# Encoder trunk on one core: the planner's TensorE starts later than the other engines, and transposes are queued later

## The chip, the cores and the metric

The kernel runs on one core of one Trainium2 chip. The metric is the device time of one execution in microseconds (us). A profiled execution has a time of its own, and beside it a span, which runs from the first to the last instruction.

The engines are called by their names in the profile: PE is TensorE (matrix products and transposes), DVE is VectorE, ACT is ScalarE, POOL is GpSimd, and SP is SyncE, which here issues nearly all transfers.

## The reference, cut to what matters

```python
for layer in range(DEPTH):                       # DEPTH = 2
    y = ab_mixer(...) if layer % 2 == 0 else cd_mixer(...)
    x = layer_norm(DN_ALPHA * x + y, ln_mix_g[layer], ln_mix_b[layer])
    f = swiglu(x, w_gate, w_up, w_down)          # (silu(x @ w_gate) * (x @ w_up)) @ w_down
    x = layer_norm(DN_ALPHA * x + f, ln_ffn_g[layer], ln_ffn_b[layer])
```

x has 256 tokens of 2048 float32 values. The feed-forward part (SwiGLU) is 5632 wide. The first layer's mixer joins a neighbourhood attention and a gated recurrence, the second layer's joins a pooling mixer and grouped-query attention. Each mixer has one projection in and one out.

## The kernel before, in words

**Tiles and products.** The 256 tokens are two tiles of 128, called tok 0 and tok 1. A float32 product is made of three matmuls (`mm3`, or `product` in the planner): each operand is split into a high part and a low part, and the three are high by low, high by high, and low by high. Their rows read `whi,xTl`, `whi,xTh` and `wlo,xTh`. Weights come from memory as pieces of 128 x 1024 values: SP issues the load into one of four `raw` buffers, ACT casts it to `whi`, and DVE takes the difference into `wlo`. One piece then serves twelve matmuls (two slices of the contraction, two tok, three products). Activations are transposed on PE (four matmuls against `ident` for 512 values of each of 128 tokens), and the result is split in the same way: ACT writes `xTh` or `yTh`, DVE writes `xTl` or `yTl`.

**Stages of a layer.** Mixer, projection out, normalisation; then `ffn`: gate and up of the first of eleven chunks of 512 hidden values (`mm_chunk`, with the SiLU on ACT at L838 and the gated product on DVE at L845, written into a view of the tile `y4h`); then `inner`; then the down projection of the last two chunks; then the normalisation that feeds the next layer.

**The planner.** `inner` computes the other ten chunks and the down projection of nine. It doesn't issue instructions as it goes, but collects operations in a `Plan`, each with its engine, its size, what it reads and writes, and the buffers (`Place`) it takes. `run` then simulates the four engines with a table of costs in ns (L88): each operation on PE is due when the ones ahead of it on PE are through, counted from zero (L150), its helpers are due that much earlier, and at each step each engine takes, among the operations that are ready, the one that is due first (L172). The order found is issued and pinned per engine with `keep_in_program_order`. The planner's clock starts at zero for every engine (L160), and it does not know of the stage ahead of it, whose instructions are still running on all engines when the first planned ones are queued.

Nine of the chunks go in units, in which six of the eight pairs of contraction slices take a form with fewer products and more additions. Its sums of activations are made by `make_forms`: two additions of `xTh` and `xTl` into `rs` (L572), four small ones into `z` (L591), then the split into `f0h` and `f0l` (L531, L535). Its sums of weights are made by `load_seven` from loads of twice the size (`rs<-in_gu`) into `sh` and `sl`.

**The end of the units.** The last unit's gated values g (ACT L664, DVE L668) of both tok are transposed outside the planner by `transpose4`, on the third and fourth piece's turn (`before`); neither they nor the products there are pinned, and the order of before has them ahead of the first product. The two banks `acc` and the two banks `mx` of the output's first half are seeded with the residual by ACT (`seed`, L413), since the first matmul adds to what stands there.

**The normalisation and the next mixer.** The second half of the output is computed tok by tok (`tok_major`). After tok 0, `norm` (L427 to L451) makes the new activations in `res`, and `flip` transposes them in four steps (L477, L478), which are not issued at once but kept in `pending`. The next `tok_major` chunk takes one step ahead of each of its pieces from piece number `FIRST_STEP` (5) on, and the rest after its last piece. Tok 0's steps are so laid into the products of tok 1, and tok 1's into the first chunk of the second layer's mixer (`cd_mixer`, its chunk 0 for keys and values). The constants of that mixer are loaded behind the last weight load of this chunk; the scale of the query norm, `nwq`, is multiplied on DVE at L1198.

Of the kernel before, what the change touches and what calls it, by code (L numbers as in the profile page):

```python
# [64 lines left out]
CD_OUT_GROUPS = (2, 0, 3, 1)  # L65
FIRST_STEP = 5
HELD = 6
FREE = 7
# [5 lines left out]
HALF = "psspsspssp"  # L74
SOON = 4000


# [12 lines left out]
class Plan:  # L90
# [11 lines left out]

    def op(self, engine, size, fn, reads=(), writes=(), times=1, lag=0, due=0):
        cost = 50 if engine == "SP" else self.COST[engine][size] * times
        i = len(self.ops)
        needs = {}
        for x in reads:
            if x in self.wrote:
                needs[self.wrote[x]] = 1
            self.read.setdefault(x, []).append(i)  # L110
        for x in writes:
            if x in self.wrote:
                needs[self.wrote[x]] = 1
            for r in self.read.pop(x, ()):
                needs.setdefault(r, 0)
            self.wrote[x] = i
        for place, _ in (*reads, *writes):
            if isinstance(place, Place) and i not in place.users:
                place.users.append(i)
        needs.pop(i, None)  # L120
        first = [p for p, _ in writes if isinstance(p, Place)]
        self.ops.append((engine, cost, size, fn, needs, first, lag, due))
        return i

    def run(self):
# [23 lines left out]
        assert len(order) == n  # L149
        due, t = [1e12] * n, 0  # L150
        pe = [i for i in range(n) if ops[i][0] == "PE"]
# [6 lines left out]
        due = [d - o[7] for d, o in zip(due, ops)]  # L158
        ready, left = [0.0] * n, [len(x) for x in needs]
        free = dict.fromkeys(("PE", "ACT", "DVE", "SP"), 0.0)  # L160
        open_ = {e: {i for i in range(n) if ops[i][0] == e and not left[i]} for e in free}
        queue, at, start, bus = 0, 0.0, [0.0] * n, 0.0
        for _ in range(n):
            best = None
            for e in free:
                if e == "PE":
                    picks = [pe[queue]] if queue < len(pe) and not left[pe[queue]] else []
                else:
                    picks = open_[e]
                if picks:  # L170
                    t = max(free[e], min(ready[i] for i in picks))
                    c = min((t, due[i], i) for i in picks if ready[i] <= t)  # L172
                    best = c if best is None else min(best, c)
            t, _, i = best
            e, cost, _, _, _, _, lag, _ = ops[i]
            open_[e].discard(i)
            queue += e == "PE"
            start[i], free[e] = t, t + cost
            end = t + cost
            if e == "SP":  # L180
                bus = max(t + 1600, bus) + ops[i][2] / 360 * 1000
                end = bus + 300
            for j in users[i]:
                x = end if needs[j][i] else t + cost
                ready[j] = max(ready[j], x + (130 + lag * needs[j][i] if ops[j][0] != e else 0))
                left[j] -= 1
                if not left[j]:
                    open_[ops[j][0]].add(j)
# [11 lines left out]
def trunk(ctx: ExitStack, tc: tile.TileContext, a, out):  # L200
# [93 lines left out]

    def mm_chunk(halves, lhs, outs, tok_major=False, after=None, before=None, seeded=False):

# [18 lines left out]
        if tok_major:  # L315
# [5 lines left out]
            for tok in range(NT):  # L321
                for i in range(n):
                    if pending and i >= FIRST_STEP:
                        step()
# [7 lines left out]
        else:  # L332
            for i, half in enumerate(halves):
                src = half[0]
                loaded.append(load_half(src, before(i) if before else ()))
                for kks in ((0,), (1,)) if before and i == 0 else ((0, 1),):
                    for tok in range(NT):
                        mms(i, tok, kks=kks)
            if after:
# [40 lines left out]
    def transpose4(src, hi, lo, ahead_by=0):  # L380
        t = trp()
        for k in range(4):
            transpose(t[:, k * P : (k + 1) * P], src[:, k * P : (k + 1) * P], ident)
        v = t.rearrange("p (k t) -> p k t", k=4)
# [131 lines left out]
    def inner(layer, sp, xT, y4, res):  # L516
# [44 lines left out]
        def make_forms(n, seven):  # L561
# [5 lines left out]
            for t in range(NT):  # L567
# [8 lines left out]
                    (),  # L576
                    [(xs, t)],
                )
            both = [(xs, 0), (xs, 1)]
# [80 lines left out]

        def gated(tok, gate, up, y):

            g = tile_of(sp, [P, NCH], f"g{tok}", 1)
            plan.op("ACT", 512, lambda: [nc.scalar.activation(g.get(), gate.get(), AF.Silu)], [(gate, 0)], [(g, 0)])  # L664
# [34 lines left out]

        def unit(w, y, down):  # L700

# [64 lines left out]
            for tok in range(NT):  # L766
                gated(tok, b[f"c{tok + 1}1"], b[f"c{tok + 1}2"], y)

# [49 lines left out]
        for units, chunks in ROUNDS:  # L818
            down = down_steps(chunks, [ys[c] for c in chunks], chunks[0] == 0)
            for c in units:  # L820
                ys[c] = new_y()
                unit(w[c], ys[c], down)
            assert next(down, None) is None
# [4 lines left out]
    def ffn(layer, xT, res, mix_pool, close_mix, keep, last):  # L828
# [54 lines left out]

        mm_chunk(some((0, 1), [(ci, j, j) for ci in range(2) for j in range(2)]), yl, outs, after=both, before=before, seeded=True)
        if cdp:
# [15 lines left out]

        mm_chunk(some((2, 3), [(ci, j, j) for j in (2, 3) for ci in range(2)]), yl, ends, tok_major=True, after=after, seeded=True)
        rings.pop()
# [310 lines left out]
    def cd_mixer(mp, consts, xT, yT):  # L1214
# [102 lines left out]
        for c, (kind, _) in enumerate(cd_plan()):  # L1317
            outs = [acc() for _ in range(NT)]
            mm_chunk([(a["cd_in"][c, n], two(2 * n)) for n in range(8)], lhs, outs, tok_major=(c == 0))
            if c == 0:  # L1320
# [174 lines left out]
```

## Time and profile before

| | |
|---|---|
| time, median of 3 runs | 2172.07 us (2170.62 to 2173.68) |
| time of the profiled execution | 2174.74 us |
| span of the profiled execution | 2173.0 us |
| mean granted TensorE clock | 0.994 of full speed |
| PE busy | 2136.8 us, 98% of the span |
| DVE busy | 1768.5 us, 81% |
| ACT busy | 1239.2 us, 57% |
| moved by DMA | 477.25 MB, 220 GB/s over the span |

A row of the timeline reads: start, duration, engine, line of the kernel, operation, out<-in, count, and in square brackets how long the engine was idle before it and what it waited for. Matmuls are pipelined: one of 128x512 has a row of 0.39 us and the next starts 0.23 us after it. A row `PE acc L557 <- ACT whi L531` in the list of waits says that the matmuls of L557 into `acc` waited for the casts of L531 into `whi`, and gives the total in us, how many times, and the longest. PEclk is the granted clock.

### The profile page before, as it was taken

Reading aid. Unit: us, or ns where it says so; the run is one execution under the profiler, and the core shown is the slowest. Engines: PE = TensorE matmul, PEld = TensorE weight load, DVE = VectorE, ACT = ScalarE, POOL = GpSimd, SP = SyncE. Lnnn points to the kernel's source line nnn. Section 1 sums busy time; section 2 is a strip of 40 time slices with the busy share of each in tenths; the row PEclk is TensorE's granted clock in tenths of the full one; section 3 lists DMA queues with packets and bytes.
Section 4 is the critical chain, followed back from the end, with each engine's and each line's share of the span. In section 5 each row is a group of like instructions: output and inputs, shape, how many; then the busy total and the mean of one; then the engine's idle time right before and its main releaser. Section 6 shows DMA issues by size and latency. Waiting matters only on the chain.

```text
span 2173.0 us, 27222 instructions
## 1 busy us (share of the span) xinstructions
PE 2136.8 (98%) x9856; PEld 1772.6 (82%) x9856; DVE 1768.5 (81%) x2226; ACT 1239.2 (57%) x1618; POOL 37.4 (2%) x43
## 2 busy tenths in 40 slices
PE   9999999999899999999999999998999999999998
PEld 7888888888788888888888788887888888888886
DVE  6885688666789999999996776675899999999976
ACT  6445534554456666666676564443566666666763
POOL 0000001000000000000000000000000000000000
PEclk9999999999999999999999999999999999999999
DMA  8555545584567777777775563554777767777754
GB/s 295 162 163 178 169 139 182 189 292 145 180 241 254 259 253 253 250 251 247 257 242 194 210 225 121 202 190 145 259 253 259 255 245 260 249 248 257 255 184 173
DMA packets 118614, 477.25 MB, mean 220 GB/s; under 512 B 13904, under 2 KB 16976, under 8 KB 103376
## 3 DMA queue, kind: packets, MB, share of 16 engines
q1 hardware_dynamic: 118480, 475.53, 63.6%
q8 instruction: 77, 1.26, 0.2%
q14 instruction: 57, 0.47, 0.1%
HBM read 473.37 MB, written 2.10 MB: 219 GB/s over the span
## 4 chain that ended last, share of the span: by engine, by line
PE 92%; DVE 4%; DMA 2%; issue 1%; ACT 1%; SPq 0%; DVEq 0%; ACTq 0%
PE un L557 33%; PE acc L398 32%; PE acc L557 19%; PE mx L398 4%; PE mx L1047 1%; PE tr L240 1%; PE un L240 1%; DMA raw<-in_down 1%; DVE wlo L244 1%; DMA rs<-in_gu 1%; DVE wlo L535 1%; ACT whi L243 0%; DMA raw<-in_cd_in 0%; PE mx L1093 0%; PE mx L1308 0%
## 5 line engine op out<-in xcount | busy, mean ns | idle before, releaser
L531 ACT CAST whi<-raw 128x1024 fp32r<-128x1024 f32 x356 | 372.2, 1050 | 211.8 <-PE acc L557 98.5
L244 DVE TENSOR_TENSOR wlo<-raw,whi 128x1024 fp32r<-128x1024 f32 (+1 forms) x297 | 360.7, 1224 | 154.9 <-ACT whi L243 152.4
L535 DVE TENSOR_TENSOR wlo<-raw,whi 128x1024 fp32r<-128x1024 f32 x356 | 430.5, 1220 | 66.4 <-ACT whi L531 62.5
L243 ACT CAST whi<-raw 128x1024 fp32r<-128x1024 f32 (+1 forms) x297 | 309.4, 1049 | 300.6 <-PE acc L398 186.7
L398 PE MATMUL acc<-whi,xTl 128*128 128x512 f32 x736 | 293.1, 398 | 5.4 <-ACT whi L243 5.1
L398 PE MATMUL acc<-whi,xTh 128*128 128x512 f32 x736 | 290.5, 395 | 0.0
L398 PE MATMUL acc<-wlo,xTh 128*128 128x512 f32 x736 | 288.1, 394 | 0.0
L557 PE MATMUL acc<-whi,yTl 128*128 128x512 f32 x576 | 225.8, 392 | 0.0
L557 PE MATMUL acc<-wlo,yTh 128*128 128x512 f32 x576 | 224.4, 390 | 0.0
L557 PE MATMUL acc<-whi,yTh 128*128 128x512 f32 x576 | 224.1, 389 | 0.0
L531 ACT CAST sh<-z 128x1024 fp32r<-128x1024 f32 x108 | 113.8, 1053 | 126.7 <-DVE z L627 73.2
L557 PE MATMUL un<-whi,xTl 128*128 128x512 f32 x460 | 180.9, 393 | 1.2 <-ACT un L731 1.1
L557 PE MATMUL un<-whi,xTh 128*128 128x512 f32 x460 | 179.2, 389 | 0.0
L557 PE MATMUL un<-wlo,xTh 128*128 128x512 f32 x460 | 179.1, 389 | 0.0
L398 PEld LDWEIGHTS acc<-whi,xTl 128*128 128x128 f32 x736 | 139.2, 189 | 33.0 <-ACT whi L243 5.8
L398 PEld LDWEIGHTS acc<-wlo,xTh 128*128 128x128 f32 x736 | 139.1, 189 | 28.4 <-DVE wlo L244 0.5
L398 PEld LDWEIGHTS acc<-whi,xTh 128*128 128x128 f32 x736 | 139.3, 189 | 26.5
L535 DVE TENSOR_TENSOR sl<-rs,sh 128x1024 fp32r<-128x1024 f32 x108 | 131.7, 1219 | 26.2 <-ACT sh L531 26.2
L531 ACT CAST sh<-rs 128x1024 fp32r<-128x1024 f32 x108 | 113.3, 1049 | 42.2 <-PE un L557 27.7
L627 DVE TENSOR_TENSOR z<-rs 128x1024 f32<-128x1024 f32 x108 | 131.7, 1220 | 1.8 <-DMA rs<-in_gu 1.0
L535 DVE TENSOR_TENSOR sl<-z,sh 128x1024 fp32r<-128x1024 f32 x108 | 131.6, 1218 | 0.0
L557 PEld LDWEIGHTS acc<-wlo,yTh 128*128 128x128 f32 x576 | 108.1, 188 | 22.7
(301 smaller groups left out, 3957.2 us busy)
## 6 DMA issues: line engine op xcount, KB each, us to landing
raw<-in_gu SPq DMA_DIRECT2D x244, 512.0 KB, 4.9
rs<-in_gu SPq DMA_DIRECT2D x108, 1024.0 KB, 4.9
raw<-in_down SPq DMA_DIRECT2D x176, 512.0 KB, 4.3
raw<-in_ab_in SPq DMA_DIRECT2D x127, 512.0 KB, 4.1
raw<-in_cd_in SPq DMA_DIRECT2D x40, 512.0 KB, 4.6
raw<-in_ab_out SPq DMA_DIRECT2D x32, 512.0 KB, 4.2
raw<-in_cd_out SPq DMA_DIRECT2D x32, 512.0 KB, 4.2
bias<-in_na_bias SPq DMA_DIRECT2D x32, 64.0 KB, 3.9
```

Of the source, the lines that this page charges most:

```text
L240: return nc.tensor.transpose(o, src, eye)
L243: nc.scalar.copy(hi, src)
L244: return nc.vector.tensor_tensor(lo, src, hi.bitcast(F32), op=sub).ins
L398: ins = nc.tensor.matmul(o, lhs[a], rhs[b], start=start and n == 0, stop=stop and n == 2, **more)
L531: plan.op("ACT", size, lambda: [nc.scalar.copy(high(), src())], reads, [(hi, at)])
L535: lambda: [nc.vector.tensor_tensor(low(), src(), high().bitcast(F32), op=sub)],
L557: yield nc.tensor.matmul(o.get(), x[i], r[j], start=begin and n == 0, stop=end and n == 2, **kw)
L627: lambda: [tt(g(), r()[:, 0:3:2], r()[:, 3:4].to_broadcast([P, 2, NCH]), op=add)],
L1047: nc.tensor.matmul(m[:, 2 * h + s, :], kk[:, h, s * P : (s + 1) * P], qq[:, h, r * P : (r + 1) * P], start=True, stop=True,)
```

## The change

The lines of the kernel move by two or three; L398 becomes L400, for instance.

```diff
+LATER = 7
+LEAD = 14000
...
-    def op(self, engine, size, fn, reads=(), writes=(), times=1, lag=0, due=0):
+    def op(self, engine, size, fn, reads=(), writes=(), times=1, lag=0, due=0, after=0):
...
-        due, t = [1e12] * n, 0
+        due, t = [1e12] * n, LEAD
...
-        ready, left = [0.0] * n, [len(x) for x in needs]
-        free = dict.fromkeys(("PE", "ACT", "DVE", "SP"), 0.0)
+        ready, left = [float(o[8]) for o in ops], [len(x) for x in needs]
+        free = {"PE": float(LEAD), "ACT": 0.0, "DVE": 0.0, "SP": 0.0}
...
-    def mm_chunk(halves, lhs, outs, tok_major=False, after=None, before=None, seeded=False):
+    def mm_chunk(halves, lhs, outs, tok_major=False, after=None, before=None, seeded=False, first_step=FIRST_STEP, pinned=0):
...
-                    if pending and i >= FIRST_STEP:
+                    if pending and i >= first_step:
...
-                        mms(i, tok, kks=kks)
+                        mms(i, tok, i < pinned, kks=kks)
...
     def transpose4(src, hi, lo, ahead_by=0):
-            transpose(t[:, k * P : (k + 1) * P], src[:, k * P : (k + 1) * P], ident)
+            tc.keep_in_program_order(transpose(t[:, k * P : (k + 1) * P], src[:, k * P : (k + 1) * P], ident))
...
     def make_forms(n, seven):       # the two additions into rs
+                    after=LEAD,
...
-        def gated(tok, gate, up, y):
-            g = tile_of(sp, [P, NCH], f"g{tok}", 1)
+        def gated(tok, gate, up, y, last=False):
+            g = edge_place(1 + tok) if last else tile_of(sp, [P, NCH], f"g{tok}", 1)
...
-                unit(w[c], ys[c], down)
+                unit(w[c], ys[c], down, c == LAST[1])
...
-        mm_chunk(some((0, 1), ...), yl, outs, after=both, before=before, seeded=True)
+        mm_chunk(some((0, 1), ...), yl, outs, after=both, before=before, seeded=True, pinned=4)
...
-        mm_chunk(some((2, 3), ...), yl, ends, tok_major=True, after=after, seeded=True)
+        mm_chunk(some((2, 3), ...), yl, ends, tok_major=True, after=after, seeded=True, first_step=LATER)
...
-            mm_chunk([(a["cd_in"][c, n], two(2 * n)) for n in range(8)], lhs, outs, tok_major=(c == 0))
+            mm_chunk([(a["cd_in"][c, n], two(2 * n)) for n in range(8)], lhs, outs, tok_major=(c == 0), first_step=LATER)
```

It has three parts. The first starts the planner's PE at 14,000 ns (`LEAD`) and its ACT, DVE and SP at zero, and holds the additions into `rs` back to the same time. The second puts the last unit's gated values into views of `y4h` instead of a buffer of their own, keeps their transposes in program order, and pins the products of the first four pieces of the last down projection, so that the transposes stand behind the first two pieces' products. The third makes the steps of `flip` begin at piece 7 instead of 5, in the second half of the down projection and in the second mixer's first chunk. The number of matmuls, casts and DVE instructions is as before.

**Place 1, the start of the planned operations, layer 0 (the same in layer 1), DVE.** L244 is the split of the stage ahead, `wlo` of L535 the planned one. Before:

```order
L244 TENSOR_TENSOR wlo<-raw,whi 128x1024 x8
L845 TENSOR_TENSOR y4h<-y4h,mx 128x512 x2
L572 TENSOR_TENSOR rs<-xTh_3818,xTl_3820 128x512
L572 TENSOR_TENSOR rs<-xTh_3819,xTl_3821 128x512
L591 TENSOR_TENSOR z<-rs 128x256
L591 TENSOR_TENSOR z<-z,rs 128x256
L591 TENSOR_TENSOR z<-rs 128x256
L591 TENSOR_TENSOR z<-rs,z 128x256
L572 TENSOR_TENSOR rs<-xTh_3818,xTl_3820 128x512
L535 TENSOR_TENSOR f0l<-z,f0h 128x1024
L535 TENSOR_TENSOR wlo<-raw,whi 128x1024 x3
```

Now:

```order
L246 TENSOR_TENSOR wlo<-raw,whi 128x1024 x8
L537 TENSOR_TENSOR wlo<-raw,whi 128x1024 x4
L848 TENSOR_TENSOR y4h<-y4h,mx 128x512 x2
L574 TENSOR_TENSOR rs<-xTh_3818,xTl_3820 128x512
L574 TENSOR_TENSOR rs<-xTh_3819,xTl_3821 128x512
L594 TENSOR_TENSOR z<-rs 128x256
```

Four planned splits now stand ahead of the gated product and of the additions. The casts on ACT move with them. Before:

```order
L243 CAST whi<-raw 128x1024 x8
L838 ACTIVATE y4h<-acc 128x512
L531 CAST f0h<-z 128x1024
L531 CAST whi<-raw 128x1024 x5
L531 CAST f1h<-z 128x1024
```

Now:

```order
L245 CAST whi<-raw 128x1024 x8
L841 ACTIVATE y4h<-acc 128x512
L533 CAST whi<-raw 128x1024 x4
L533 CAST f0h<-z 128x1024
L533 CAST whi<-raw 128x1024 x3
L533 CAST f1h<-z 128x1024
```

Four of the planned casts have moved ahead of `f0h`. On SP ten loads of `raw` now stand ahead of the first load of `rs` instead of eight.

**Place 2, the end of the units, layer 0 (the same in layer 1), PE.** `un` are the last unit's products, `tr` the transposes of its gated values, `acc` and `mx` the output's first half. Before:

```order
L557 MATMUL un<-wlo,xTh_3819 128x512
L240 MATMUL tr<-ident,g_9854 128x128 x4
L240 MATMUL tr<-ident,g_9862 128x128 x4
L398 MATMUL acc<-whi,yTl 128x512
L398 MATMUL acc<-whi,yTh 128x512
```

Now, at the point where the transposes went (24 matmuls into `acc` stand between the last `un` and the first row):

```order
L400 MATMUL acc<-whi,yTh 128x512
L400 MATMUL acc<-wlo,yTh 128x512
L242 MATMUL tr<-ident,y4h 128x128 x4
L400 MATMUL mx<-whi,yTl 128x512
L400 MATMUL mx<-whi,yTh 128x512
```

The first transposes have moved behind 24 matmuls, and the second behind 12 more. On ACT, L413 is the seed of a bank. Before:

```order
L243 CAST whi<-raw 128x1024 x2
L664 ACTIVATE g_9854<-un 128x512
L664 ACTIVATE g_9862<-un 128x512
L243 CAST whi<-raw 128x1024
L413 ACTIVATE acc<-res_3802 128x512
L413 ACTIVATE mx<-res_3802 128x512
```

Now:

```order
L245 CAST whi<-raw 128x1024 x2
L667 ACTIVATE y4h<-un 128x512 x2
L245 CAST whi<-raw 128x1024 x4
L415 ACTIVATE acc<-res_3802 128x512
L415 ACTIVATE mx<-res_3802 128x512
```

Four casts of weights instead of one stand between the SiLU and the first seed.

**Place 3, the start of the second layer's mixer, DVE.** `xTl` are the low parts of the transposed activations of tok 0, L421 the statistics of tok 1. Before:

```order
L451 TENSOR_TENSOR res_3802<-res_3802,bet 128x512 x2
L244 TENSOR_TENSOR wlo<-raw,whi 128x1024 x2
L478 TENSOR_TENSOR xTl_9896<-tr,xTh_9894 128x512
L244 TENSOR_TENSOR wlo<-raw,whi 128x1024
L478 TENSOR_TENSOR xTl_9896<-mx,xTh_9894 128x512
L478 TENSOR_TENSOR xTl_9896<-tr,xTh_9894 128x512
L421 BN_STATS st_9899<-mx 128x6
L244 TENSOR_TENSOR wlo<-raw,whi 128x1024
L478 TENSOR_TENSOR xTl_9896<-mx,xTh_9894 128x512
L427 BN_AGGR mv<-st_9899 128x2
L1198 TENSOR_SCALAR nwq<-nwq 128x128
```

Now:

```order
L453 TENSOR_TENSOR res_3802<-res_3802,bet 128x512
L246 TENSOR_TENSOR wlo<-raw,whi 128x1024 x2
L480 TENSOR_TENSOR xTl_9894<-tr,xTh_9892 128x512
L1201 TENSOR_SCALAR nwq<-nwq 128x128
L423 BN_STATS st_9897<-mx 128x6
L246 TENSOR_TENSOR wlo<-raw,whi 128x1024
L480 TENSOR_TENSOR xTl_9894<-mx,xTh_9892 128x512
L480 TENSOR_TENSOR xTl_9894<-tr,xTh_9892 128x512
L429 BN_AGGR mv<-st_9897 128x2
L480 TENSOR_TENSOR xTl_9894<-mx,xTh_9892 128x512
```

The product of `nwq` has moved up from behind the last `xTl` to behind the first. On SP the load of `nwq` no longer stands behind a load of weights.

More of the change, by code (lines that the diff above doesn't have):

```diff
@@ L121, in op @@
         first = [p for p, _ in writes if isinstance(p, Place)]
-        self.ops.append((engine, cost, size, fn, needs, first, lag, due))
+        self.ops.append((engine, cost, size, fn, needs, first, lag, due, after))
         return i
@@ L174, in run @@
             t, _, i = best
-            e, cost, _, _, _, _, lag, _ = ops[i]
+            e, cost, _, _, _, _, lag, _, _ = ops[i]
             open_[e].discard(i)
@@ L698, in whole, with unit @@
                 gated(tok, gate[tok], up[tok], y)
-        def unit(w, y, down):
+        def unit(w, y, down, last):
             run = lambda: next(down, None)
@@ L766, in unit @@
             for tok in range(NT):
-                gated(tok, b[f"c{tok + 1}1"], b[f"c{tok + 1}2"], y)
+                gated(tok, b[f"c{tok + 1}1"], b[f"c{tok + 1}2"], y, last)
         def down_steps(chunks, ys, start):
@@ L882, in before @@
             return ()
-        mm_chunk(some((0, 1), [(ci, j, j) for ci in range(2) for j in range(2)]), yl, outs, after=both, before=before, seeded=True)
+        mm_chunk(some((0, 1), [(ci, j, j) for ci in range(2) for j in range(2)]), yl, outs, after=both, before=before, seeded=True, pinned=4)
         if cdp:
@@ L900, in after @@
                 norms[0](tok, nxt, out if last else None, {j: ends[tok][j] for j in (2, 3)})
-        mm_chunk(some((2, 3), [(ci, j, j) for j in (2, 3) for ci in range(2)]), yl, ends, tok_major=True, after=after, seeded=True)
+        mm_chunk(some((2, 3), [(ci, j, j) for j in (2, 3) for ci in range(2)]), yl, ends, tok_major=True, after=after, seeded=True, first_step=LATER)
         rings.pop()
```

## The prediction, made before the change was run

> **What bounds the kernel now.** I read the busy times of the page first, then the chain that ended last, then PE's list of waits.
>
> ```profile
> PE 2136.8 (98%) x9856; PEld 1772.6 (82%) x9856; DVE 1768.5 (81%) x2226; ACT 1239.2 (57%) x1618; POOL 37.4 (2%) x43
> ...
> PE 92%; DVE 4%; DMA 2%; issue 1%; ACT 1%; SPq 0%; DVEq 0%; ACTq 0%
> ...
> PE acc L557 <- ACT whi L531: 11.5, 2, 5.7
> PE acc L398 <- ACT whi L243: 5.1, 2, 4.8
> PE tr L240 <- DVE res L451: 3.0, 2, 2.3
> PE tr L240 <- DVE g L668: 2.4, 2, 1.2
> PE acc L557 <- DVE wlo L535: 1.5, 2, 0.8
> ```
>
> PE is never idle for long, and 92% of the chain is PE's. The number of matmuls doesn't change, so the change can move the time only through PE's holes and what follows them. The second wait row is at the kernel's start, which the change leaves alone. The other four are the change's three places: 11.5 + 1.5 us where planned work begins (twice, once in each layer), 2.4 where the units end (twice), 3.0 where the second mixer begins.
>
> **Place 1, the planned start: a gain.** PE in layer 0, then in layer 1:
>
> ```profile
> 556.88 0.39 PE L398 MATMUL mx<-wlo,xTh 128*128 128x512 f32 x1
> 562.99 0.80 PE L557 MATMUL acc<-whi,xTl 128*128 128x512 f32 x1 [5.72 <-ACT whi L531]
> 564.99 0.80 PE L557 MATMUL acc<-wlo,xTh 128*128 128x512 f32 x1 [0.78 <-DVE wlo L535]
> ...
> 577.69 0.39 PE L557 MATMUL acc<-wlo,xTh 128*128 128x512 f32 x1
> 577.92 1.03 PE L240 MATMUL un<-ident,y4h 128*128 128x128 f32 x8
> ...
> 1500.81 0.39 PE L398 MATMUL mx<-wlo,xTh 128*128 128x512 f32 x1
> 1506.94 0.80 PE L557 MATMUL acc<-whi,xTl 128*128 128x512 f32 x1 [5.74 <-ACT whi L531]
> ...
> 1521.00 1.03 PE L240 MATMUL un<-ident,y4h 128*128 128x128 f32 x8
> ```
>
> Matmuls at full rate start 0.227 us apart (577.69 to 577.92). From the last `mx` to the transposes there are 48 planned matmuls (four pieces of twelve), 10.88 us at that rate. Layer 0 takes 577.92 − 557.11 = 20.81, layer 1 1521.00 − 1501.04 = 19.96. So 9.9 and 9.1 are lost, 19.0 in all: 13.0 in waits (11.5 + 1.5 in the list), the rest in matmuls at half rate behind them. The other engines in layer 0:
>
> ```profile
> 534.25 34.78 SPq L541 DMA_DIRECT2D raw<-in_gu  x8
> ...
> 560.95 1.04 ACT L531 CAST f0h<-z 128x1024 fp32r<-128x1024 f32 x1 [20.89 <-DVE z L591]
> 561.90 3.88 ACT L531 CAST whi<-raw 128x1024 fp32r<-128x1024 f32 x4
> ...
> 563.72 3.49 DVE L535 TENSOR_TENSOR wlo<-raw,whi 128x1024 fp32r<-128x1024 f32 x3
> ...
> 550.00:560.00 10.00, 7.27 (x33) 5.68 (x31) 3.24 (x6) 0.00 (x0) 0.00 (x0) 0.99 0.00 0
> 560.00:570.00 10.00, 6.23 (x14) 4.45 (x15) 9.68 (x15) 5.60 (x6) 0.00 (x0) 0.50 0.36 120
> ```
>
> The casts that PE lacks stood behind `f0h` on ACT, which slept 20.89 us until `z` was there; `z` needs the gated product, and that needs the last `mx`. The loads were not the reason: in 550 to 560 DMA moved nothing (last column 0). In the new order the four casts and four splits stand ahead of the gated product, behind loads that began at 534.25 and need only buffers that the up matmuls free as they go. A cast takes 0.97 (3.88 / 4), a split 1.16 (3.49 / 3); four fit between 540 and 557, while ACT is idle. In layer 1 the fourth buffer comes free only with the last `mx`, so its split ends near 1501.0 + 0.97 + 1.16 = 1503.2, but the fourth piece is wanted 3 x 2.72 = 8.2 us after the start, at 1509.2. No wait is left at the start: **−19.0**.
>
> What is late next is DVE. PE comes 9.9 and 9.1 us earlier, but the gated product and the additions behind it gain only the four splits (4.6 us) in layer 0, and only 2.3 in layer 1, where the product now waits for the late fourth split. DVE is left 5.3 and 6.8 us further behind PE than before. What covers that is its idle time at the end of the first 65 us of planned work:
>
> ```profile
> 606.00:624.00 18.00, 18.00 (x85) 14.99 (x84) 11.00 (x12) 9.04 (x10) 0.00 (x0) 1.00 0.58 192
> ```
>
> DVE (third pair) is busy 11.0 of 18.0: 7.0 us of idle, which holds 5.3, and just holds 6.8. Until then every buffer margin must bear the lag; pieces five to eight, by the same cast and split times from z's end, come 1.5 to 2.8 us before PE wants them. I take nothing off and keep the loss of it as a rival.
>
> **Place 2, the units' end: a loss, twice.** Layer 0, PE, ACT and SP, and the landings of `raw` from 1162 to 1190:
>
> ```profile
> 1173.61 0.60 PE L240 MATMUL tr<-ident,g 128*128 128x128 f32 x4
> 1175.40 0.63 PE L240 MATMUL tr<-ident,g 128*128 128x128 f32 x4 [1.19 <-DVE g L668]
> 1175.79 0.47 PE L398 MATMUL acc<-whi,yTl 128*128 128x512 f32 x1
> 1176.10 0.39 PE L398 MATMUL acc<-whi,yTh 128*128 128x512 f32 x1
> ...
> 1171.09 0.60 ACT L664 ACTIVATE g<-un 128x512 f32<-128x512 f32 x1 [0.76 <-PE un L557]
> 1172.35 1.05 ACT L243 CAST whi<-raw 128x1024 fp32r<-128x1024 f32 x1 [0.67 <-DMA raw<-in_down]
> 1173.31 0.59 ACT L413 ACTIVATE acc<-res 128x512 f32<-128x512 f32 x1
> ...
> 1169.12 1.69 SPq L281 DMA_DIRECT2D raw<-in_down  x2
> ...
> DMA to landing us min/median/max: 3.2/4.3/5.5
> ```
>
> Call E the end of the last unit product, 1173.61. Before, two transposes and the wait for g put the first `acc` matmul at E + 2.18. Now that matmul is first and needs only its pieces and its seed. But the seed, done by 1173.9 before, stands behind four casts instead of one. The fourth cast's load is the second of the two issued from 1169.12, at 1169.12 + 1.69 − 0.33 = 1170.5; with 4.3 it lands at 1174.8, the cast ends at 1175.7, the seed at 1176.3: a hole of 2.7 us (2.45 with the landing of 3.2, 4.0 with 5.5). The transposes then cost their 2 x 0.36 later on, so one end loses 2.7 − 2.18 + 0.72 = 1.2.
>
> A hole of this length may also cost the clock. Nearest rows: the hole of 1.8 us between 1173.61 and 1175.40 was followed by full rate (the next matmul's row has 0.39 us); the rows of place 3 show one of 2.26 and more, ahead of 1231.91, in a window with a clock of 0.83, about 1.5 us lost. So the price is 0 to 1.5, and 2.7 is nearer to the second: I take 1.3. Two ends: 2 x (1.2 + 1.3) = **+5.0** (bounds 2 and 8).
>
> **Place 3, the second mixer: a small gain.** PE, DVE, SP, and the window 1230 to 1240:
>
> ```profile
> 1208.55 0.39 PE L398 MATMUL acc<-whi,yTl 128*128 128x512 f32 x1
> ...
> 1216.24 0.63 PE L240 MATMUL tr<-ident,res 128*128 128x128 f32 x4 [0.72 <-DVE res L451]
> ...
> 1222.56 0.50 PE L398 MATMUL acc<-whi,xTl 128*128 128x512 f32 x1 [0.22 <-DVE xTl L478]
> ...
> 1231.91 0.76 PE L240 MATMUL tr<-ident,res 128*128 128x128 f32 x4 [2.26 <-DVE res L451]
> ...
> 1221.82 0.68 DVE L478 TENSOR_TENSOR xTl<-tr,xTh 128x512 fp32r<-128x512 f32 x1
> ...
> 1228.23 0.23 DVE L1198 TENSOR_SCALAR nwq<-nwq 128x128 f32<-128x128 f32 x1 [0.90 <-DMA nwq<-in_d_q_norm]
> ...
> 1210.64 0.33 SPq L281 DMA_DIRECT2D raw<-in_cd_in  x1
> ...
> 1230.00:1240.00 10.00, 8.09 (x37) 6.72 (x38) 7.06 (x11) 5.49 (x10) 0.00 (x0) 0.83 0.35 122
> ```
>
> Against the 0.36 of an undisturbed group of transposes, the three rows with waits cost 0.9, 0.6 and 2.4 us; at the clock of 0.83 another 1.5 go: 5.4 in all. Two pieces of six matmuls are 2 x 1.36 = 2.7 us by which both sets of steps move back, more than the 0.72 and 2.26 waited, so those two vanish. But three of tok 0's four steps now stand right ahead of the mixer's first product, which needs the first `xTl`. If P is the start of tok 1's products (1208.55), PE gets there at P + 48 x 0.227 + 4 x 0.36 = P + 12.3. The first `xTl` keeps as many splits ahead of it as before, when it ended at 1222.4 = P + 13.9, and the statistics of tok 1 now stand ahead of it behind the split of the load issued at 1210.64 (P + 2.1): P + 13.6 to P + 16.3, with a landing of 4 to 7 us, the casts and splits behind it. The new wait is 1.3 to 4.0; I take 2.2, nearer the row of before, 0.8 for the clock behind it (0 to 1.5), and 0.4 for `nwq` (0 to 1.4: its load is issued 0.4 earlier, but it is queued four DVE instructions ahead of where it waited 0.90). −5.4 + 3.4 = **−2.0** (bounds −4 and +1.5).
>
> **The sum.** −19.0 + 5.0 − 2.0 = −16.0. The profiled execution took 2174.74, 2.67 over the median; 2174.74 − 16.0 = 2158.7 in its terms, and against the median 2172.07 − 16.0 = **2156**.
>
> **The rivals.**
>
> *The new holes leave the clock alone.* Then place 2 costs 2 x 1.2 = 2.4, and place 3 gives −5.4 + 2.6 = −2.8: −19.0 + 2.4 − 2.8 = −19.4, so 2152.7. For it speaks the hole of 1.8 at 1175.40, after which nothing was slow; against it the hole before 1231.91. The Trainium skill, "TensorE: Matmul & The Clock Gate" (Why this matters for your kernels), asks for no idle gaps over about 3 us, by which holes of 2.7 would pass; the clock of 0.83 behind 1231.91 doesn't agree.
>
> *The seeds come in time.* If PE goes straight from the unit into `acc`, each end gains 2.18 − 0.72 = 1.5, and with nothing new at place 3 the sum is −19.0 − 3.0 − 5.4 = −27.4: 2144.7. The four casts ahead of the seed in the new order speak against it.
>
> *DVE takes the head start back.* If DVE's idle 7.0 us come too late for a buffer that it frees, only what DVE itself gained stays: −4.6 − 2.3 + 5.0 − 2.0 = −3.9, so 2168.2. For it: DVE is busy 9.68 of 10 in 560 to 570. Against: among the waits of PE over half a microsecond, those above, none is for DVE's work inside the units.
>
> *Slower: the transposes' low parts wait for a late load, at both ends.* In the new order the first `yTl` of the last chunk stands on DVE behind seven splits, the last of them of the eleventh piece. That piece's buffer is freed by the seventh piece's split, which follows the six seeds: 1175.7 + 6 x 0.53 + 0.97 + 1.16 = 1181.0 = E + 7.4; with a landing of 4.3, 0.97 and 1.16 for cast and split and 0.6 for itself `yTl` is there at E + 14.5, just when PE (E + 2.7, 48 matmuls, two transposes: E + 14.3) wants it. Each us that this load is later goes straight to PE. Landings of 4.3 + 6.7 = 11.0 make two losses of 6.7 and two clocks of 1.3, 16.0: from there on the kernel is slower. At 12 it is 2172.07 − 16.0 + 2 x (7.7 + 1.3) = 2174. In 1162 to 1190 no landing is over 5.5, but half a chunk later:
>
> ```profile
> DMA to landing us min/median/max: 3.1/4.6/10.9
> ```
>
> That the change doesn't do what it says is out: the order's rows show the four casts and splits ahead.
>
> **How the numbers follow.** My forecast 0.60, clock untouched 0.22, seeds in time 0.05, DVE 0.08, slower 0.05. The forecast alone spans −16.0 with +3 at place 2, and −2 to +3.5 at place 3, from 2151 to 2162. The range 2149 to 2164 takes in the second case and part of the DVE case, with 0.15 to 0.2 left out. A change of under 0.2% (4.3 us) can't be told from none here, so faster means below 2167.7: the first three cases and half of the fourth, 0.91; the same 0.05, slower 0.04.
>
> **What would show it.** Right: the row `acc <- whi` of the planned start is gone from the waits, 48 matmuls take some 11 us after the last `mx`; at the units' end the first `acc` matmul waits 2 to 3 us for a cast or a seed (L415), with a lower clock behind it; the first matmul of the second mixer waits for `xTl`, and the row `tr <- res` is gone. Wrong: waits in the units for DVE's `wlo`, `z` or `sl` in the first 100 us of planned work; a wait for `yTl` at the end; or the old hole, shorter, at the start.

## The result, and the profile after

| | before | changed |
|---|---|---|
| median | 2172.39 us (2170.62 to 2173.68) | 2156.01 us (2155.03 to 2157.57) |
| ratio | | 0.9926 (0.9909 to 0.9943) |
| median, in a later group of runs | 2175.81 us | 2159.01 us |
| ratio there | | 0.9921 (0.9907 to 0.9934) |
| span of the profiled execution | 2173.0 us | 2153.9 us |

The change makes the kernel 16.4 us faster, 2156.0 us where 2156 was forecast. The total is the forecast's; two of its terms are not, as the places show, so that the close agreement of the total is partly luck.

The page and PE's list of waits of the changed kernel; in the list, line 415 is the seed:

```profile
PE 2130.5 (99%) x9856; PEld 1768.5 (82%) x9856; DVE 1767.9 (82%) x2226; ACT 1239.1 (58%) x1618; POOL 41.9 (2%) x43
...
PE acc L400 <- ACT whi L245: 5.6, 3, 4.8
PE acc L400 <- ACT acc L415: 5.0, 2, 2.6
PE un L559 <- ACT un L734: 1.0, 2, 0.5
PE un L242 <- DVE g L671: 0.4, 2, 0.2
PE acc L400 <- DVE xTl L480: 0.2, 1, 0.2
```

The 11.5 and 1.5 us of the planned start are gone, and so are the waits for `res` and for g ahead of `tr`. One row is new: 5.0 us for the seed.

**Place 1.** PE, ACT and DVE in layer 0, and the window that answers to the one in which DVE was idle for 7 us:

```profile
556.87 0.39 PE L400 MATMUL mx<-wlo,xTh 128*128 128x512 f32 x1
557.10 0.39 PE L559 MATMUL acc<-whi,xTl 128*128 128x512 f32 x1
...
567.98 1.03 PE L242 MATMUL un<-ident,y4h 128*128 128x128 f32 x8
...
554.35 1.05 ACT L533 CAST whi<-raw 128x1024 fp32r<-128x1024 f32 x1 [1.67 <-PE mx L400]
560.82 1.05 ACT L533 CAST f0h<-z 128x1024 fp32r<-128x1024 f32 x1 [5.41 <-DVE z L594]
...
555.44 1.23 DVE L537 TENSOR_TENSOR wlo<-raw,whi 128x1024 fp32r<-128x1024 f32 x1 [1.49 <-ACT whi L533]
...
596.00:614.00 18.00, 18.00 (x86) 14.97 (x85) 13.86 (x16) 8.98 (x10) 0.00 (x0) 1.00 0.71 248
```

The planned matmul follows the last `mx` by 0.23 us, and the transposes come 10.88 us later: nothing is lost. The fourth cast waits only for a buffer that the up matmuls free. `f0h` comes no earlier than before (560.82 against 560.95), yet PE no longer stands behind it. DVE's idle time in the 18 us window has shrunk from 7.0 to 4.1 us: the lag is there, smaller than the 5.3 us of the forecast, and is absorbed.

**Place 2.** PE at the end of the units in layer 0, then ACT there, then PE in layer 1, then the two windows (the last figure but two is the granted clock):

```profile
1163.44 0.39 PE L559 MATMUL un<-wlo,xTh 128*128 128x512 f32 x1
1166.43 0.50 PE L400 MATMUL acc<-whi,yTl 128*128 128x512 f32 x1 [2.60 <-ACT acc L415]
...
1161.64 2.93 ACT L245 CAST whi<-raw 128x1024 fp32r<-128x1024 f32 x3
1164.83 1.04 ACT L245 CAST whi<-raw 128x1024 fp32r<-128x1024 f32 x1 [0.26 <-DMA raw<-in_down]
1165.78 0.59 ACT L415 ACTIVATE acc<-res 128x512 f32<-128x512 f32 x1
...
2094.07 0.39 PE L559 MATMUL un<-wlo,xTh 128*128 128x512 f32 x1
2096.89 0.53 PE L400 MATMUL acc<-whi,yTl 128*128 128x512 f32 x1 [2.43 <-ACT acc L415]
2097.22 0.62 PE L400 MATMUL acc<-whi,yTh 128*128 128x512 f32 x1
...
1160.00:1170.00 10.00, 7.33 (x31) 5.41 (x31) 6.36 (x8) 8.98 (x14) 0.00 (x0) 1.00 0.76 239
2090.00:2100.00 10.00, 7.57 (x28) 5.68 (x27) 6.97 (x7) 8.73 (x13) 0.00 (x0) 0.86 0.67 214
```

The seed stands behind four casts, the fourth of which waits for its load. From the last `un` to the first `acc` matmul 2.99 and 2.82 us pass, 2.76 and 2.59 more than the usual 0.23. Behind the first hole the clock stays at 1.00; behind the shorter second one it is 0.86, and the matmuls start 0.42 apart (2097.22 to the next at 2097.64 and on to 2100.65). Why the longer one is spared is in the last section.

**Place 3.** PE from the start of tok 1's products to the second layer's mixer, and DVE:

```profile
1200.59 0.39 PE L400 MATMUL acc<-whi,yTl 128*128 128x512 f32 x1
...
1213.41 0.50 PE L400 MATMUL acc<-whi,xTl 128*128 128x512 f32 x1
1216.57 0.50 PE L400 MATMUL acc<-whi,xTl 128*128 128x512 f32 x1 [0.15 <-DVE xTl L480]
...
1202.12 0.26 DVE L429 BATCH_NORM_AGGREGATE mv<-st 128x2 f32<-128x24 f32 x1
...
1212.66 0.69 DVE L480 TENSOR_TENSOR xTl<-tr,xTh 128x512 fp32r<-128x512 f32 x1
1213.96 0.23 DVE L1201 TENSOR_SCALAR nwq<-nwq 128x128 f32<-128x128 f32 x1 [0.60 <-DMA nwq<-in_d_q_norm]
```

The first `xTl` is there at 1213.35, and PE goes on at 1213.41, 0.23 us later than the transposes ahead of it would have let it (they start at 1212.82 and take 0.36). Little is left of the 1.3 to 4.0 us of waiting that were forecast, and `nwq` still waits but holds PE up no more.

For the rest, four stretches of PE's timeline are compared, in us, each from the start of one row to the start of another, so that each holds the same matmuls in every kernel. The end of the units is taken as 0.23 us after the start of the last `un` matmul.

- *start 0* and *start 1*: from the last `mx` of the up projection to the transposes of the first chunk's values (556.88 to 577.92 before), in layer 0 and 1; 11.11 with no loss
- *end 0*: from the end of the units in layer 0 to the first transposes of the second mixer's attention, with places 2 and 3
- *end 1*: from the end of the units in layer 1 to the last matmul, with place 2 alone

| | start 0 | start 1 | end 0 | end 1 |
|---|---|---|---|---|
| before, first profile | 21.04 | 20.19 | 125.52 | 45.59 |
| before, second and third | 21.07, 20.27 | 21.46, 20.50 | 125.78, 126.75 | 45.58, 45.59 |
| changed, two profiles | 11.11, 11.11 | 11.11, 11.12 | 122.66, 123.10 | 48.60, 49.21 |
| first part alone, two | 11.11, 11.11 | 11.12, 11.11 | 122.87, 122.20 | 45.69, 45.63 |
| second part alone | 20.72 | 20.43 | 123.62 | 49.11 |
| third part alone | 20.72 | 21.42 | 123.37 | 45.63 |
| first and third | 11.11 | 11.11 | 122.54 | 45.52 |
| changed, seeds ahead | 11.11 | 11.11 | 121.73 | 44.25 |
| seeds ahead, steps from 5 and 6 | 11.11 | 11.12 | 121.02 | 44.26 |

### The profile page after: what moved, and what is told of

Read it like the earlier page. It is cut to its first block, busy times and chain, and to the rows that moved or that the text cites. A ratio compares the mean times of both kernels' runs of the same rounds, so it can differ in the third digit from the quotient of the medians.

```text
span 2153.9 us, 27234 instructions
## 1 busy us (share of the span) xinstructions
PE 2130.5 (99%) x9856; PEld 1768.5 (82%) x9856; DVE 1767.9 (82%) x2226; ACT 1239.1 (58%) x1618; POOL 41.9 (2%) x43
## 4 chain that ended last, share of the span: by engine, by line
PE 93%; DVE 3%; DMA 2%; ACT 1%; issue 1%; SPq 0%; DVEq 0%; ACTq 0%
PE un L559 33%; PE acc L400 32%; PE acc L559 19%; PE mx L400 4%; PE mx L1050 1%; PE tr L242 1%; PE un L242 1%; DMA raw<-in_down 1%; DVE wlo L246 1%; DMA raw<-in_cd_in 1%; ACT whi L245 0%; DVE wlo L537 0%; DMA rs<-in_gu 0%; PE mx L1096 0%; DVE sl L537 0%
## 5 line engine op out<-in xcount | busy, mean ns | idle before, releaser
L400 PE MATMUL acc<-whi,xTl 128*128 128x512 f32 x736 | 292.4, 397 | 5.7 <-ACT whi L245 5.6
L400 PE MATMUL acc<-whi,xTh 128*128 128x512 f32 x736 | 289.6, 393 | 0.0
L400 PE MATMUL acc<-wlo,xTh 128*128 128x512 f32 x736 | 287.2, 393 | 0.1
L400 PEld LDWEIGHTS acc<-whi,xTl 128*128 128x128 f32 x736 | 138.7, 188 | 34.0 <-ACT whi L245 6.6
L400 PEld LDWEIGHTS acc<-wlo,xTh 128*128 128x128 f32 x736 | 138.5, 188 | 28.4 <-DVE wlo L246 0.7
L400 PEld LDWEIGHTS acc<-whi,xTh 128*128 128x128 f32 x736 | 138.9, 189 | 26.4
```

The lines of the kernel that those rows point to most:

```text
L400: ins = nc.tensor.matmul(o, lhs[a], rhs[b], start=start and n == 0, stop=stop and n == 2, **more)
```

## The experiments

The edits are shown against the changed kernel. Ratios are against the kernel before, timed on the same chip in the same group, with 95% intervals. The first part, the second, the third and the moved seeds were one group; the four runs beside the changed kernel's second measurement were another. The median of before differs from group to group (2172.39, 2176.42, 2175.81), so times are compared within one.

### The first part alone

```diff
 LATER = 5                       # steps as before; LEAD = 14000 stays
-            g = edge_place(1 + tok) if last else tile_of(sp, [P, NCH], f"g{tok}", 1)
+            g = tile_of(sp, [P, NCH], f"g{tok}", 1)
-            tc.keep_in_program_order(transpose(...))
+            transpose(...)
-        mm_chunk(..., before=before, seeded=True, pinned=4)
+        mm_chunk(..., before=before, seeded=True)
```

> The first part of the change alone (planner's PE starts at 14,000 ns, additions into rs held back); the unit's end and the steps of the flips as before. Theory A (the terms of the prediction add up): -19.0 us against before, 2153 us; the 48 matmuls after the last mx take 10.9 us in both layers, and from the first planned transposes to the end of the units nothing is lost in return (595.7 us in layer 0, as before). Theory B (the profiled execution of before lost more at the planned start than its usual execution, since how long the half rate lasts behind a hole differs from one execution to the next): the timed gain is smaller than the profile says, -15 to -17, since only the 13.0 us of waits are certain and the 6 us of half rate are not. Rival (VectorE gives the head start back): -7.

Measured: 2155.76 us against 2176.42, ratio 0.9906 (0.9892 to 0.9919), −20.7 us; again, beside the changed kernel:

> The first part alone, again, beside the changed kernel. Theory (the second part costs 2 x 3 us at the units' ends and gives 2 to 4 back at the second mixer, the third part nothing): 2 to 4 us faster than the changed kernel. Rival (the parts add up as predicted, +5 and -2): 3 us faster as well, but with the waits at the second mixer worth 5.4 us, as in the profile before.

2155.41 against 2175.81, ratio 0.9910 (0.9896 to 0.9923), −20.4, where the changed kernel had 2159.01 (0.9921, 0.9907 to 0.9934). Theory A's −19.0 lies in the interval of the first measurement (−17.6 to −23.5). The starts lose nothing, and the units take 597.6 and 596.4 us in the one profile, 597.6 and 595.3 in the other. That is 1.9 over the 595.7 that theory A had for layer 0, but not a cost of the early start: in the five profiles with the planner as before a layer's units take 595.4 to 598.2 us, in the seven with the early start 595.2 to 598.4. VectorE gives nothing like 12 us back, so that rival is out. So is theory B: 9.1 to 10.4 us are lost at each start in all three profiles of the kernel before and in both kernels that leave the planner as it was.

The first part alone is by 3.6 us of medians (2159.01 − 2155.41) the better kernel, as the table has it: *end 1* is 2.9 to 3.6 us shorter, *end 0* the same. The intervals of the two ratios overlap, so it is the stretches that tell them apart. Something unforeseen is in *end 0*: the order there is that of before on PE and DVE, and still it takes 122.2 to 122.9 us instead of 125.5 to 126.8. Two rows of PE, the window behind them, and `nwq` on DVE:

```profile
1220.79 0.39 PE L400 MATMUL acc<-wlo,xTh 128*128 128x512 f32 x1
1223.14 0.63 PE L242 MATMUL tr<-ident,res 128*128 128x128 f32 x4 [1.96 <-DVE res L453]
...
1220.00:1230.00 10.00, 8.04 (x44) 6.45 (x43) 8.35 (x14) 6.25 (x12) 0.82 (x1) 1.00 0.46 161
...
1219.46 0.23 DVE L1201 TENSOR_SCALAR nwq<-nwq 128x128 f32<-128x128 f32 x1 [0.60 <-DMA nwq<-in_d_q_norm]
```

The hole ahead of tok 1's transposes is still there, but 2.12 us instead of 2.41, and the clock behind it is 1.00, not 0.83. Tok 0's wait for `res`, 0.72 us before, is gone from the list of waits (one wait of 2.0 us, where before has two of 3.0 together). The two further profiles of before were taken to see whether that is the rule.

### The kernel before, profiled again

No edit.

> The kernel before, profiled again, to see how much of its loss changes from one execution to the next. Theory (the hole ahead of tok 1's first transposes at the second mixer lies just where it does or doesn't bring half rate: 1.9 and 2.1 us brought none in the runs with the first part alone, 2.4 did in the profile before): the planned start loses 9 to 10.5 us in each layer again; at the second mixer, from tok 1's products to the first transposes of the attention, 90.6 us when the hole there is over 2.3 us and 87 to 89 when it is shorter. Rival (the planned start itself varies by 2 us and more): there the difference to the profile before.

> The same, a third profile of the kernel before: as for the second.

PE and the window of the second profile, and `nwq`:

```profile
1229.99 0.39 PE L398 MATMUL acc<-wlo,xTh 128*128 128x512 f32 x1
1233.06 1.09 PE L240 MATMUL tr<-ident,res 128*128 128x128 f32 x4 [2.68 <-DVE res L451]
...
1230.00:1240.00 10.00, 7.32 (x34) 5.83 (x33) 7.84 (x12) 5.17 (x8) 0.74 (x1) 0.83 0.43 154
...
1229.38 0.23 DVE L1198 TENSOR_SCALAR nwq<-nwq 128x128 f32<-128x128 f32 x1 [1.32 <-DMA nwq<-in_d_q_norm]
```

Here the hole is 2.84 us in both, with half rate behind it, and *end 0* takes 125.8 and 126.8. The hole follows the landing of `nwq`: 5.6 us after its issue in the first profile (hole 2.41), 6.0 in the second (2.84), 5.3 and 5.1 in those of the first part alone (2.12 and 1.87). Each 0.1 us of landing is some 0.1 us of hole, and the half rate that followed the three longer ones costs some 1.7 more. Why `nwq` lands earlier in the kernel with the first part isn't settled; the two were not profiled in the same group, for one thing. The planned start loses 20.3 to 21.5 less 11.1 again.

### The second part alone

```diff
 LEAD = 0                        # the planner as before
 LATER = 5                       # the steps as before
```

> The second part alone (gated values of the last unit in views of y4h, their transposes pinned behind the first 24 products). Theory A: a loss of 1.2 us per end by the hole in front of the first acc matmul, and 0 to 1.5 us of half rate behind each, so +2.4 to +5 us, 2174.5 to 2177; holes of 2.5 to 2.9 us ended by the seed of L415. Rival (the seeds come in time when the planner's start is as before): no hole, -3 us, 2169.

Measured: 2180.29 us, ratio 1.0017 (1.0008 to 1.0026): slower by 3.7 us (1.7 to 5.7). The holes at the ends are 2.87 and 2.49 us, half rate follows both, and *end 1* takes 49.11, 3.5 more than before. *End 0* takes 2 to 3 us less. The window 1220 to 1230, where before has the wait for `xTl` and the hole for `res`:

```profile
1220.00:1230.00 10.00, 10.00 (x52) 8.28 (x51) 9.97 (x17) 4.38 (x7) 0.82 (x1) 1.00 0.75 248
```

PE is busy for all of it; its list of waits has no row for `res` and none for `xTl`, and that with the steps at piece 5, as before. ACT, DVE and SP do not stand still in PE's hole and come to the second mixer earlier by PE's clock: the statistics of tok 0 are closed (`mv<-st` on DVE) 0.94 us after the start of tok 1's products, where the kernel before needs 2.7 to 3.6.

### The third part alone, and with the first

```diff
 LEAD = 0                        # third part alone; 14000 in the other
-            g = edge_place(1 + tok) if last else tile_of(sp, [P, NCH], f"g{tok}", 1)
+            g = tile_of(sp, [P, NCH], f"g{tok}", 1)
-            tc.keep_in_program_order(transpose(...))
+            transpose(...)
-        mm_chunk(..., before=before, seeded=True, pinned=4)
+        mm_chunk(..., before=before, seeded=True)
```

> The third part alone (steps of the flips from piece 7 on in the two chunks). By the prediction -2.0 us (2170), with a new wait of 1.3 to 4.0 us for the first xTl. By the profile after, where this place gained 4.4 us: -4 (2168), with the waits for res gone and no wait over 0.3 us for xTl. Rival (what gained at this place came from the second part, which moved the loads of the second mixer, and not from the later steps): 0 or slower, with a wait for xTl of over 1 us.

> The first and the third part, without the second. Theory (the later steps only trade the waits for res against one for xTl, unless the hole at the unit's end gives VectorE the time): a wait of 1.5 to 2.5 us for the first xTl, none for res, and the time of the first part alone within 2 us. Rival (prediction: the later steps gain 2 to 4 us by themselves): 2 to 4 us faster than the first part alone, no wait for xTl over 0.5.

The third part alone: 2176.16 us, ratio 0.9995 (0.9986 to 1.0004), no difference to be seen; of the times expected for it, only the rival's fits. With the first: 2154.82, ratio 0.9910 (0.9897 to 0.9924), that of the first part alone. PE of the third part alone, at the mixer's first product, and a row of the waits of the first and third:

```profile
1223.29 0.60 PE L242 MATMUL mx<-ident,res 128*128 128x128 f32 x4
1225.69 0.50 PE L400 MATMUL acc<-whi,xTl 128*128 128x512 f32 x1 [1.80 <-DVE xTl L480]
```

```profile
PE acc L400 <- DVE xTl L480: 1.8, 1, 1.8
```

This is the size of wait that was forecast for the changed kernel, 1.80 and 1.75 us where 2.2 was taken. DVE shows where it is from. Its rows in the third part alone:

```profile
1213.27 0.26 DVE L429 BATCH_NORM_AGGREGATE mv<-st 128x2 f32<-128x24 f32 x1
...
1221.56 3.48 DVE L246 TENSOR_TENSOR wlo<-raw,whi 128x1024 fp32r<-128x1024 f32 x3
1224.96 0.68 DVE L480 TENSOR_TENSOR xTl<-tr,xTh 128x512 fp32r<-128x512 f32 x1
```

From the closing of the statistics to the first `xTl` DVE never idles, so the distance is the work between them: 11.69 us here, with three splits in a row ahead of `xTl`, five in all. In the changed kernel it is 10.54 (1202.12 to 1212.66), with four, as in the kernel before (10.56). The fifth split is 1.15 us of the wait. The rest is when the statistics are closed: 2.2 us after the start of tok 1's products here (with the first part 2.15), 1.53 and 0.93 in the two profiles of the changed kernel. So the later steps trade the waits for `res` against one for `xTl`. Alone, they shorten *end 0* by 2 to 3 us, since they leave a hole of 2.0 us without half rate instead of 2.4 to 2.8 with it; the timed runs don't show that gain.

### The seeds ahead of the casts

```diff
-                nc.scalar.activation(psum, ...)          # in seed
+                return nc.scalar.activation(psum, ...)
...
-        for j in range(2):
-            for tok in range(NT):
-                seed(tok, j, outs[tok][j], 1.0)
+        first = [seed(tok, j, outs[tok][j], 1.0).ins for j in range(2) for tok in range(NT)]
...
                 flips.pop(0)()
+            if i == 2:
+                ahead[:] = first[:2]     # the next four pieces' casts and splits
+                held[0] = 4              # are issued behind these two
```

> The whole change, and the seeds of the output's first half ahead of the third to sixth cast of weights on ScalarE at the unit's end. If the four casts ahead of the seed make the hole there, it goes in both layers: -2.8 and -2.6 us of waits against the changed kernel, and the half rate behind one of them (about 1.5): -5.5 to -7, so 2149 to 2150.5 us. If something else holds the first product (its weights, the gated values), the hole stays and the time too, 2156.

ACT and PE of this kernel at the end of the units in layer 0, and PE at the mixer's first product:

```profile
1163.03 0.60 ACT L667 ACTIVATE y4h<-un 128x512 f32<-128x512 f32 x1 [0.76 <-PE un L559]
1163.52 0.60 ACT L415 ACTIVATE acc<-res 128x512 f32<-128x512 f32 x1
1164.04 0.59 ACT L415 ACTIVATE mx<-res 128x512 f32<-128x512 f32 x1
...
1165.32 0.39 PE L559 MATMUL un<-wlo,xTh 128*128 128x512 f32 x1
1165.55 0.39 PE L400 MATMUL acc<-whi,yTl 128*128 128x512 f32 x1
...
1213.88 0.51 PE L400 MATMUL acc<-whi,xTl 128*128 128x512 f32 x1 [1.89 <-DVE xTl L480]
```

Measured: 2154.09 us, ratio 0.9896 (0.9882 to 0.9909), 22.3 us under before. The hole is gone in both layers, and *end 1* is 44.25, the shortest so far: 1.3 under before, 4.4 to 5.0 under the changed kernel. So the four casts made the hole, as forecast. The changed kernel wasn't in this group; by the ratios (0.9926 and 0.9921 for it, 0.9896 here) this one is 5.4 to 6.5 us lower, where 5.5 to 7 was expected. In layer 0 a part goes again: the wait for `xTl` is back with 1.89 us. The statistics are closed 2.29 us after the start of tok 1's products, since the other engines have no hole in which to get ahead, and the order of this kernel has the fifth split ahead of `xTl` (11.70 us between the two).

### The seeds ahead, and the steps from piece 5 and 6

```diff
 # on top of the one before
-        mm_chunk(some((2, 3), ...), ..., first_step=LATER)
+        mm_chunk(some((2, 3), ...), ..., first_step=5)
-            mm_chunk(..., tok_major=(c == 0), first_step=LATER)
+            mm_chunk(..., tok_major=(c == 0), first_step=6)
```

> The first and the second part with the seeds ahead of the casts, and the steps of the flips from piece 5 on in the down projection and from piece 6 on in the second mixer's first chunk. Theory: the unit ends cost 11.9 us for the first 48 products and their transposes, as with the seeds moved before; the first xTl comes in time since it isn't behind the late splits, the wait for res of tok 0 is 0.5 to 1.5 us, of tok 1 under 1.5 us: 1 to 3 us under the kernel with moved seeds and both steps at 7, 5 to 8 us under the changed kernel, the fastest of all. Rival (the second mixer's start is bound by VectorE's total work there): the same as with both steps at 7.

> The changed kernel as it is, a second time, so that the others of this group are compared with it on one chip. 16 to 17 us under before (ratio 0.9926); its profile with a hole of 2.5 to 2.9 us at each unit end, each followed by 0 or about 3.4 us of half rate, and no wait over 0.3 us for xTl.

Measured: 2151.95 us, ratio 0.9891 (0.9878 to 0.9905), beside the changed kernel's 2159.01 (0.9921): 7.1 us of medians, and the fastest of its group, each run below each of the others'. From the seeds ahead alone (0.9896, in the other group) the times don't tell it apart. Two rows of its waits:

```profile
PE tr L242 <- DVE res L453: 1.3, 2, 0.7
...
PE acc L400 <- DVE xTl L480: 0.2, 1, 0.2
```

Four splits stand ahead of the first `xTl` again (10.55 us). What is left are 1.3 us in two waits for `res`, with full rate behind both, and 0.2 for `xTl`. *End 0* is 121.02, 5 us under before.

## Why the prediction was right or wrong

**Place 1: right, to 0.1 us.** Forecast −19.0, against the first profile of before (21.04 + 20.19) − 2 x 11.11 = 19.0. Over the three profiles of before the loss is 18.6 to 20.3. The step on DVE held as well: no wait inside the units for its lag.

**Place 2: the hole right, the clock too small.** Forecast a hole of 2.7 us (2.45 to 4.0), measured 2.76 and 2.59, 2.40 and 2.89 in the second profile. What was mis-sized is "I take 1.3" for the half rate. Layer 1 shows it by itself: 44.25 us with no hole, 48.60 with one of 2.59, so 1.8 for the clock, 49.21 − 44.25 − 2.89 = 2.1 in the second profile and 49.11 − 44.25 − 2.49 = 2.4 with the second part alone. One end costs 3.0 to 3.6 us instead of 2.5. It isn't paid at every hole: none behind the one of 2.76. The hole of 1.8 us that spoke for a lower price holds 0.36 us of transposes, so it was one of 1.4.

**Place 3: wrong in size, by a step that can be named.** "The first `xTl` keeps as many splits ahead of it as before" was right: four, 10.54 us from the closing of the statistics in the changed kernel and 10.56 before. Wrong was where that chain starts. "P + 13.6 to P + 16.3" took for granted that DVE closes the statistics no earlier after P, the start of tok 1's products, than before (2.71 us). But place 2, one section earlier in the same prediction, holds PE back by 3 us and doesn't hold the loads, casts and splits that stand ahead of the statistics. They are closed at P + 1.53 and P + 0.93, and `xTl` is there at P + 12.8 and P + 12.2, when PE is at P + 12.6 (12.3 in the forecast). The wait for the first `xTl` is 0.2 us in the one profile and none in the other, instead of 2.2, with no clock behind it, and tok 1's hole is gone. In the three profiles with a hole at the units' end the statistics are closed 0.9 to 1.5 us after P, in the nine without 1.5 to 3.6. The first part alone, without a hole, is at 1.5 and 2.0, so not all of the head start is shown to be the hole's. Two terms were added that are not independent: places 2 and 3 of layer 0 were forecast at +2.5 − 2.0 = +0.5 and measured (*end 0*) at −2.4 to −4.1. How much of that the two places gain is open: the first part alone, which has neither, takes 122.2 to 122.9 there, the same as the changed kernel.

**The sum.** By the stretches, −19.0 − 2.9 + 3.0 = −18.9 between the first two profiles, whose spans differ by 19.1. The forecast of −16.0 was therefore 3 us off in the profile's terms, by *end 0*. Against the medians it was right to 0.4 us, and that is luck: the profiled execution of before took 2.67 us more than the median it was set beside, and that of the changed kernel 0.36 less (2155.65). Where in the program the other runs of before are faster by these 2.67 us, no trace shows; half rate that they might be spared at the second mixer (1.7) would be most of it, but that is only argued.

**The rivals.** *The new holes leave the clock alone*: out, since 5 of the 6 holes at units' ends (two profiles of the changed kernel, one of the second part alone) were followed by half rate; the sixth was spared by its place, as the last section has it. *The seeds come in time*: not in this change; made so by an edit, each end gains as it said (1.3 us against 1.5). *DVE takes the head start back* and *the late load*: out; no wait for `yTl` shows in the list.

## What to carry to other kernels

When a planner or a scheduler orders several engines, ask what the first instruction of each waits for at the seam to the stage before: here one cast whose input needed the last matmul held up four that did not, 9.5 us each time. A hole on the bounding engine lets all the others run ahead, so holes that follow each other on it may not be added up: here a later wait went with the first hole there, and came back, 1.89 us long, when the first hole was mended (1.15 us of it by one more split in the way). Run the parts of a change apart; of this one's three the first carries it, the second costs as long as the seeds stand behind the casts, and the third does nothing that could be measured.

## What the runs showed of the hardware

The granted clock fell to half behind much shorter holes of PE than expected, and the length of a hole alone doesn't decide it. Counting as hole the time beyond the usual spacing, 1.87, 1.99, 2.04, 2.12 and 2.13 us brought no half rate; 2.40, 2.41, 2.49, 2.59, 2.84, 2.84, 2.87 and 2.89 did, and of those above 2.4 only one of 2.76 did not.

What does decide it can be read from the traces. In each of the twelve, every stretch at one clock between two changes is a multiple of 3.41 us long: 3.41 and 47.79 us (14 x 3.41) in the first profile of the changed kernel, 269.65 us (79 x 3.41) in the first of before. So the clock changes on a grid of 3.41 us. Here are four windows of that grid in the first profile of the changed kernel, around its two holes, and then two in the second profile, around the hole of 2.40. PE's busy time in a window is the second figure:

```profile
1161.97:1165.38 3.41, 1.86 (x9) 1.20 (x7) 2.80 (x3) 3.15 (x4) 0.00 (x0) 1.00 0.50 147
1165.38:1168.79 3.41, 2.29 (x9) 1.59 (x10) 3.02 (x4) 3.41 (x7) 0.00 (x0) 1.00 0.87 299
2093.81:2097.22 3.41, 0.98 (x4) 0.48 (x3) 3.41 (x5) 3.32 (x5) 0.00 (x0) 1.00 0.50 173
2097.22:2100.64 3.42, 3.42 (x9) 2.48 (x8) 2.02 (x3) 3.18 (x6) 0.00 (x0) 0.50 0.74 246
...
1165.72:1169.13 3.41, 1.52 (x5) 0.97 (x6) 3.41 (x5) 3.41 (x7) 0.00 (x0) 1.00 0.69 183
1169.13:1172.54 3.41, 3.41 (x9) 2.64 (x8) 1.97 (x2) 2.68 (x4) 0.00 (x0) 0.50 0.69 262
```

The hole of 2.76 us is cut in two by the grid, and PE is busy for 1.86 and 2.29 us of its two windows. The hole of 2.59 us lies in one window, which has 0.98, and the window behind it is at half rate; so is the one behind 1.52. In all twelve traces a window at full rate in which PE was busy for 1.52 us or less was followed by one at half rate, and none with 1.58 us or more was. The five shorter holes are cut as well, with 1.6 us at most in one window, so the runs don't show that their shortness spared them. Matmuls in a window at half rate start 0.42 us apart instead of 0.23, so with PE busy throughout one such window costs some 1.7 us (an estimate, half of 3.41).

The Trainium skill, "TensorE: Matmul & The Clock Gate" (What's actually happening), has the clock fall after at least one idle window of some 3.4 us, with windows that run freely. The length of the window and its free running agree with these traces, but no whole idle window was needed here: 0.98 and 1.52 us of matmuls in one did not keep the clock up.

A load of 64 KB, `nwq`, so had a part in whether some 1.7 us of PE time were lost. In the three profiles of before and the two of the first part alone it took 5.1 to 6.0 us to land, DVE waited for it with tok 1's normalisation queued behind, and the hole that this made on PE, 1.87 to 2.84 us long, had half rate behind it in three of the five.
